# Attention with grouped queries: contiguous casts, rows transposed two at a time, and a shorter VectorE exponent

## Chip, cores, metric

One core of a Trainium2 chip. The metric is device time in microseconds (us); executions of a kernel lie within some 2% of each other, and each comparison uses the fast runs of both kernels made on the same chip in the same rounds. A profiled span is one execution's, and up to 6 us from the timed median of the same kernel.

## The reference

Eight batches, eight query heads in two groups, two key/value heads, sequence 1024, head dimension 64; softmax(q k^T / 8) v, in float32:

```python
scores = scale * np.matmul(q_group, k_group.transpose(0, 1, 3, 2))
scores_max = np.max(scores, axis=-1, keepdims=True)
attn = np.exp(scores - scores_max)
attn = attn / (np.sum(attn, axis=-1, keepdims=True) + 1e-08)
output[:, q_start:q_end, :, :] = np.matmul(attn, v_group)
```

## The kernel before

Scores are made transposed: a cell is one 128 x 512 block (128 keys, 512 queries), 8 cells a job, 128 jobs. A cell's exponents are made either by ScalarE (two cells at once, kind A) or by VectorE (kind D): a first pass writes bits from PSUM as uint16, and for four cells at once a chain of passes adds a quadratic correction. A small planner, run when the kernel is built, decides which cell goes where and in which order each engine works; transfers are recorded at "plan time of first use minus a lead". Parts that matter (cuts marked, and the chain in short form):

```python
def cast(key, src):                       # fp32 -> bf16, DRAM to DRAM, issued by GpSimd
    scr = scr_pool.tile([S, G * D], BF16, name="scr")
    nc.gpsimd.dma_start(out=scr.rearrange("s (g d) -> s g d", g=G),
                        in_=src.rearrange("g s d -> s g d"))      # runs of 64 elements
def transpose(key, dst, n):               # issued by SyncE
    nc.sync.dma_start_transpose(out=dst[:, rows], in_=scratch[key][rows, :])
def place_k(b, g):                        # GpSimd copies
    nc.gpsimd.tensor_copy(out=ksets[b % 2][half, g, :], in_=kT[b][half, :])
def place_v(b, g):
    nc.gpsimd.tensor_copy(out=vsets[b % 2][:, g, :, 0:D], in_=vstage.pop((b, g)))
...                                       # VectorE chain of four cells
    z = pd & 0xFF
    y = z * (CURVE_A / 512) + CURVE_B / 2
    y = z * y
    z = pd >> 1
    pd = z + y
```

The softmax here doesn't subtract the row's maximum and nothing guards it: scores larger than these inputs give would overflow.

## Time and profile before

| | before |
|---|---|
| time, us | 447.93 (447.81 to 448.04) |
| span of the profiled run, us | 449.2 |
| DVE (VectorE) / ACT (ScalarE) / PE (TensorE) busy | 93% / 87% / 86% |
| granted TensorE clock | 0.979 |

The prediction below shows the lines of this profile and reads them: VectorE is the bound, and it is lengthened where GpSimd works. Two more lines of it matter later, from the waits of GpSimd (what waited, for what; us in all, times, longest):

```profile
POOL vset L281 <- DMA vstage<-in_v_dram: 173.8, 7, 38.3
POOL vset L281 <- PE aps L324: 66.5, 2, 34.9
```

The trace shows GpSimd working in the order of its program: a query cast starts at 214.31 us, right behind the last of two value copies that had waited 31.6 us for TensorE's scores and 2.1 us for its output products. So the casts stood behind copies that waited for loads and for TensorE: the copies held the casts back, although nobody had asked them to.

### The profile page before, as it was taken

The page shows a single profiled execution, that of the slowest core. Times are in us where ns is not written, and L with a number is a line of the kernel's source. Part 1 is how long each engine was busy: PE and PEld are TensorE (multiplying, and loading weights), DVE is VectorE, ACT ScalarE, POOL GpSimd, SP SyncE. Part 2 cuts the span into 40 slices and gives each one's busy share as a digit, 9 for nine tenths or more (in the row PEclk, how much of TensorE's full clock was granted, in tenths as well). Part 3 has the DMA queues.
Part 4 walks back from the last instruction along what each step waited for, and adds up shares of the span by engine and source line. Part 5 has one row for each costly group of instructions (what it writes and reads, how often), then busy time and mean ns, then how long its engine had stood idle before and what let it go on. Part 6 is the DMA issues. An engine that isn't in the chain of part 4 may idle for free.

```text
span 449.2 us, 12594 instructions
## 1 busy us (share of the span) xinstructions
PE 386.4 (86%) x5136; PEld 234.2 (52%) x5136; DVE 416.8 (93%) x699; ACT 389.7 (87%) x417; POOL 111.3 (25%) x80
## 2 busy tenths in 40 slices
PE   1989878999689998898799998899989987998972
PEld 1445545655456555464455565546545655564661
DVE  2699999899999999999999999999999999999976
ACT  1799988899689998899799999899998998999940
POOL 7600263003620039000820035400380016100000
PEclk9999999899899999999999999999999999999986
DMA  9922579226992399934992359933999357923221
GB/s 163 110 44 43 114 99 157 61 63 106 114 135 63 64 136 120 116 73 101 105 153 57 76 110 109 130 75 80 135 105 109 83 112 100 111 58 71 61 49 35
DMA packets 210649, 42.77 MB, mean 95 GB/s; under 512 B 210592, under 2 KB 210592, under 8 KB 210592
## 3 DMA queue, kind: packets, MB, share of 16 engines
q1 hardware_dynamic: 132160, 32.01, 39.2%
q0 software_dynamic: 78432, 9.96, 37.5%
q8 instruction: 40, 0.66, 0.7%
q14 instruction: 17, 0.14, 0.1%
HBM read 25.17 MB, written 26.74 MB: 116 GB/s over the span
## 4 chain that ended last, share of the span: by engine, by line
DVE 55%; PE 20%; DMA 9%; ACT 6%; issue 6%; SPq 3%; POOL 1%; ACTq 0%; POOLq 0%; DVEq 0%
DVE pd L344 11%; DVE y L375 10%; DVE pd L387 9%; PE aps L324 9%; DMA qT<-scr 7%; PE ops L395 6%; DVE ost L410 6%; DVE y L365 6%; ACT pa L335 6%; DVE z L377 5%; PE dps L324 4%; DVE z L359 4%; DVE rec L408 3%; SPq L256 2%; DMA kT<-scr 1%
## 5 line engine op out<-in xcount | busy, mean ns | idle before, releaser
L335 ACT ACTIVATE pa<-aps 128x1024 bf16<-128x1024 f32 x415 | 387.4, 1044 | 32.5 <-PE aps L324 30.5
L324 PE MATMUL aps<-qT,kset 128*128 128x512 bf16 x830 | 250.0, 383 | 21.3 <-ACT pa L335 11.4
L395 PEld LDWEIGHTS <-pa 128*128 128x128 bf16 x3320 | 137.0, 99 | 65.1 <-DVE ost L410 11.5
L395 PE MATMUL ops<-vset,pa 128*128 128x65 bf16 x3320 | 145.7, 195 | 3.0 <-DVE ost L410 3.0
L344 DVE TENSOR_SCALAR pd<-dps 128x512 uint16<-128x512 f32 x194 | 126.0, 682 | 6.3 <-PE dps L324 6.2
L324 PEld LDWEIGHTS <-kset 128*128 128x128 bf16 x1024 | 85.6, 98 | 85.4 <-issue 41.8
L281 POOL CAST vset<-vstage 128x512 bf16<-128x512 f32 x16 | 18.2, 1140 | 242.3 <-DMA vstage<-in_v_dram 173.8
L248 POOL DMA_DIRECT2D scr<-in_q_dram x31 | 77.8, 2948 | 0.0
L324 PE MATMUL dps<-qT,kset 128*128 128x512 bf16 x194 | 65.2, 386 | 2.4 <-DMA qT<-scr 1.1
L375 DVE TENSOR_TENSOR y<-z,y 128x2048 f16<-128x2048 uint16 (+1 forms) x49 | 61.6, 1257 | 1.7
L387 DVE TENSOR_TENSOR pd<-z,y 128x2048 uint16<-128x2048 uint16 (+1 forms) x49 | 60.3, 1231 | 1.5
L395 PEld LDWEIGHTS <-pd 128*128 128x128 bf16 x776 | 32.1, 98 | 52.0 <-DVE pd L387 42.2
L395 PE MATMUL ops<-vset,pd 128*128 128x65 bf16 x776 | 38.2, 195 | 24.0 <-DVE pd L387 23.5
L410 DVE TENSOR_TENSOR ost<-ops,rec 128x256 f32<-128x256 f32 x128 | 54.4, 425 | 4.4
L359 DVE TENSOR_SCALAR z<-pd 128x2048 uint16<-128x2048 uint16 (+1 forms) x49 | 40.1, 818 | 0.0
L365 DVE TENSOR_SCALAR y<-z 128x2048 f16<-128x2048 uint16 (+1 forms) x49 | 39.7, 810 | 0.4
L377 DVE TENSOR_SCALAR z<-pd 128x2048 uint16<-128x2048 uint16 (+1 forms) x49 | 36.1, 736 | 1.7
L408 DVE RECIPROCAL rec<-ops 128x4 f32<-128x4 f32 x128 | 22.2, 174 | 6.9 <-PE ops L395 6.9
L248 POOL DMA_DIRECT2D scr<-in_k_dram x7 | 28.6, 4079 | 0.0
L265 POOL COPY kset<-kT 64x1024 bf16<-64x1024 bf16 x14 | 16.1, 1151 | 28.8 <-DMA kT<-scr 28.4
L301 PE MATMUL dps<-ident,h 128*128 128x128 bf16 x16 | 2.1, 309 | 8.3 <-DVE h L298 8.3
L307 ACT COPY qT<-dps 128x1024 bf16<-128x1024 bf16 x1 | 1.0, 1012 | 8.3 <-PE dps L301 8.3
(12 smaller groups left out, 10.6 us busy)
## 6 DMA issues: line engine op xcount, KB each, us to landing
out_dram<-ost SPq DMA_DIRECT2D x128, 128.0 KB, 2.7
scr<-in_q_dram POOLq DMA_DIRECT2D x31, 256.0 KB, 7.8
vstage<-in_v_dram SPq DMA_DIRECT2D x16, 256.0 KB, 4.4
qT<-scr SPq DMA_TRANSPOSE x124, 2.7
scr<-in_k_dram POOLq DMA_DIRECT2D x7, 256.0 KB, 10.1
f<-in_k_dram SPq DMA_DIRECT2D x2, 256.0 KB, 3.6
f<-in_q_dram SPq DMA_DIRECT2D x2, 256.0 KB, 4.7
kT<-scr SPq DMA_TRANSPOSE x28, 2.6
```

What stands on the lines that cost most here:

```text
L248: nc.gpsimd.dma_start(out=scr.rearrange("s (g d) -> s g d", g=G), in_=src.rearrange("g s d -> s g d"),)
L324: nc.tensor.matmul(dst, lhsT=ksets[b % 2][:, g, c * 128 : (c + 1) * 128], rhs=qT[(b, j)][:, qb * QBS : (qb + 1) * QBS], start=True, stop=True,
L335: nc.scalar.activation(out=pt[:, 0:m], in_=psum.pop(("A", n))[:, 0:m], func=AF.Exp, scale=scale)
L344: nc.vector.tensor_scalar(out=groups[g][:, slot], in0=psum.pop(cell), scalar1=bits_scale, scalar2=bits_bias, op0=ALU.mult, op1=ALU.add,)
L359: nc.vector.tensor_scalar(out=z, in0=pd, scalar1=0xFF, scalar2=None, op0=ALU.bitwise_and)
L365: nc.vector.tensor_scalar(out=y, in0=temps[g][0], scalar1=CURVE_A / 512.0, scalar2=CURVE_B / 2.0, op0=ALU.mult, op1=ALU.add,)
L375: nc.vector.tensor_tensor(out=y, in0=z, in1=y, op=ALU.mult)
L377: nc.vector.tensor_scalar(out=temps[g][0], in0=pd, scalar1=1, scalar2=None, op0=ALU.logical_shift_right,)
L387: nc.vector.tensor_tensor(out=pd, in0=z, in1=y, op=ALU.add)
L395: nc.tensor.matmul(ops_of[s][:, qs, :], lhsT=p_of[cell][:, qs * 128 : (qs + 1) * 128], rhs=vsets[b % 2][:, g, c, :], start=opens and qs == ...
L408: nc.vector.reciprocal(out=rec, in_=o[:, :, D])
L410: nc.vector.tensor_tensor(out=ost, in0=o[:, :, 0:D], in1=rec.unsqueeze(2).to_broadcast([128, NQS, D]), op=ALU.mult,)
```

## The change

Its intent: take the shift out of the VectorE chain (steps of 7 bits need none); make casts contiguous, a whole batch of queries in one; free GpSimd of copies, so that it doesn't lengthen VectorE; make the start shorter. A transpose now reads two sequence rows of one head as one row of 128, so a job is the even or the odd queries of a head, keys are held for both sides, and keys and values are placed by SyncE's DMAs. The diff is shortened:

```diff
-    LIVE_A, LIVE_D, PENDING = 24, 7, 8
+    LIVE_A, LIVE_D, PENDING, ONLY_A = 26, 6, 8, 14     # the last 14 cells on ScalarE
...
-    jobs = [(b, j, qb, g) ...]
+    jobs = [(b, h, side) for b in range(B) for h in range(H) for side in range(2)]
...
-        nc.gpsimd.dma_start(out=scr.rearrange("s (g d) -> s g d", g=G), in_=src.rearrange("g s d -> s g d"))
+        nc.gpsimd.dma_start(out=scr.rearrange("n (p f) -> (n p) f", f=1024),
+                            in_=src.rearrange("n (p s) d -> (n p) (s d)", s=1024 // D))
...
-    def place_k(b, g):
-        nc.gpsimd.tensor_copy(out=ksets[b % 2][half, g, :], in_=kT[b][half, :])
+    def place_k(b, g, side, parity):
+        nc.sync.dma_start(out=ksets[b % 2][side * D : (side + 1) * D, g, side, parity * HALF : ...],
+                          in_=kT[(b, g)][parity * D : (parity + 1) * D, :])
+    def place_v(b, g):      # two nc.sync.dma_start, even and odd rows, from the cast values
...
-        z = pd & 0xFF; y = z * (CURVE_A / 512) + CURVE_B / 2; y = z * y; z = pd >> 1; pd = z + y
+        z = pd & 0x7F; y = z * (CURVE_A / 128) + CURVE_B;     y = z * y;              pd = pd + y
...
+            at(th - 7.0 + n, transpose_q, b, h, n)        # leads: us of the plan ahead of first use
+            at(th - 13.0 + n, transpose_k, b, g, n)       # first head of a group
+            at(th - 8.5, place_k, b, g, side, parity); at(th - 6.0, place_v, b, g)
+            at(t0 - 28.0, cast_kv, b); at(t0 - 24.0, cast_q, b, 0, H)      # a whole batch
```

More of the change, by code (lines that the diff above doesn't have):

```diff
@@ L18, in make_plan @@
 def make_plan(nj, nkc):
-    QK, PV, EXP, P1, NORM = 0.214, 0.142, 0.925, 0.665, 0.64
-    CHAIN = (0.60, 0.60, 1.08, 0.60, 1.08)
+    QK, PV, EXP, P1, NORM = 0.214, 0.143, 0.925, 0.605, 0.57
+    CHAIN = (0.73, 0.73, 1.26, 1.26)
     FROM_PE, FROM_ACT, FROM_DVE = 0.28, 0.18, 0.12
-    LIVE_A, LIVE_D, PENDING = 24, 7, 8
+    LIVE_A, LIVE_D, PENDING, ONLY_A = 26, 6, 8, 14
     INF = 1e9
@@ L53, in make_plan @@
                 ta = max(pe, min(a_free))
-            if pending < PENDING and (cur or live["D"] < LIVE_D):
+            if pending < PENDING and nxt < n - ONLY_A and (cur or live["D"] < LIVE_D):
                 td = max(pe, min(bank))
@@ L70, in make_plan @@
                 best = min(best or (INF,), (max(dve, q[0][0]), p, kind, 0))
-        if cur and nxt >= n and not p1q:
+        if cur and nxt >= n - ONLY_A and not p1q:
             best = min(best or (INF,), (dve, 9, "flush", 0))
@@ L180 @@
     G = k.shape[1]
-    NPAIR = H // G
+    HPG = H // G
     NKC = S // 128
     QBS = 512
-    NQB = S // QBS
+    HALF = S // 2
+    NHC = NKC // 2
     NQS = QBS // 128
@@ L188 @@
     scale = 1.0 / math.sqrt(D)
-    bits_scale = 256.0 * scale * math.log2(math.e)
-    bits_bias = 256.0 * 127.0
-    jobs = [
-        (b, j, qb, g)
-        for b in range(B)
-        for j in range(NPAIR)
-        for qb in range(NQB)
-        for g in range(G)
-    ]
+    bits_scale = 128.0 * scale * math.log2(math.e)
+    bits_bias = 128.0 * 127.0
+    jobs = [(b, h, side) for b in range(B) for h in range(H) for side in range(2)]
     plan = make_plan(len(jobs), NKC)
@@ L205 @@
     scr_pool = ctx.enter_context(
-        tc.tile_pool(name="scr", bufs=4, space=bass.MemoryType.DRAM)
+        tc.tile_pool(name="scr", bufs=2, space=bass.MemoryType.DRAM)
     )
     first_pool = ctx.enter_context(tc.tile_pool(name="firstp", bufs=1))
-    qT_pool = ctx.enter_context(tc.tile_pool(name="qTpool", bufs=4))
+    qT_pool = ctx.enter_context(tc.tile_pool(name="qTpool", bufs=6))
     kT_pool = ctx.enter_context(tc.tile_pool(name="kTpool", bufs=2))
-    vstage_pool = ctx.enter_context(tc.tile_pool(name="vstage", bufs=2 * G))
-    pa_pool = ctx.enter_context(tc.tile_pool(name="papool", bufs=24))
-    pd_pool = ctx.enter_context(tc.tile_pool(name="pdpool", bufs=7))
+    vstage_pool = ctx.enter_context(tc.tile_pool(name="vstage", bufs=G))
+    pa_pool = ctx.enter_context(tc.tile_pool(name="papool", bufs=26))
+    pd_pool = ctx.enter_context(tc.tile_pool(name="pdpool", bufs=6))
     tmp_pool = ctx.enter_context(tc.tile_pool(name="tmppool", bufs=2))
@@ L234 @@
         vsets.append(vs)
-        ks = const_pool.tile([128, G, S], BF16, name=f"kset{s}")
-        for g in range(G):
-            nc.gpsimd.memset(ks[(1 - g) * D : (2 - g) * D, g, :], 0.0)
+        ks = const_pool.tile([128, G, 2, S], BF16, name=f"kset{s}")
+        for side in range(2):
+            nc.vector.memset(ks[(1 - side) * D : (2 - side) * D, :, side, :], 0.0)
         ksets.append(ks)
@@ L242, with cast @@
     scratch = {}
-    vstage = {}
-    def cast(key, src):
-        scr = scr_pool.tile([S, G * D], BF16, name="scr")
+    def cast(key, src, n):
+        scr = scr_pool.tile([n, S * D], BF16, name=f"scr_{key[0]}{n}")
         nc.gpsimd.dma_start(
-            out=scr.rearrange("s (g d) -> s g d", g=G),
-            in_=src.rearrange("g s d -> s g d"),
-        )
-        scratch[key] = scr
+            out=scr.rearrange("n (p f) -> (n p) f", f=1024),
+            in_=src.rearrange("n (p s) d -> (n p) (s d)", s=1024 // D),
+        )
+        return scr
@@ L254, in transpose, with cast_q, cast_kv @@
+    def cast_q(b, h, n):
+        scr = cast(("q",), q[b, h : h + n], n)
+        for i in range(n):
+            scratch[("q", b, h + i)] = scr[i]
+    def cast_kv(b):
+        for name, src in (("k", k), ("v", v)):
+            scr = cast((name,), src[b], G)
+            for g in range(G):
+                scratch[(name, b, g)] = scr[g]
     def transpose(key, dst, n):
         rows = slice(n * PIECE, (n + 1) * PIECE)
-        nc.sync.dma_start_transpose(out=dst[:, rows], in_=scratch[key][rows, :])
@@ L258, in transpose_k @@
-    def transpose_k(b, n):
+        src = scratch[key].rearrange("(r c) -> r c", c=2 * D)
+        nc.sync.dma_start_transpose(out=dst[:, rows], in_=src[rows, :])
+    def transpose_k(b, g, n):
         if n == 0:
-            kT[b] = kT_pool.tile([128, S], BF16, name="kT")
-        transpose(("k", b), kT[b], n)
-    def place_k(b, g):
-        half = slice(g * D, (g + 1) * D)
-        nc.gpsimd.tensor_copy(out=ksets[b % 2][half, g, :], in_=kT[b][half, :])
-    def transpose_q(b, j, n):
-        if n == 0:
-            qT[(b, j)] = qT_pool.tile([128, S], BF16, name="qT")
-        transpose(("q", b, j), qT[(b, j)], n)
@@ L272, in load_v, with transpose_q @@
-    def load_v(b):
+            kT[(b, g)] = kT_pool.tile([128, HALF], BF16, name="kT")
+        transpose(("k", b, g), kT[(b, g)], n)
+    def place_k(b, g, side, parity):
+        nc.sync.dma_start(
+            out=ksets[b % 2][
+                side * D : (side + 1) * D, g, side, parity * HALF : (parity + 1) * HALF
+            ],
+            in_=kT[(b, g)][parity * D : (parity + 1) * D, :],
+        )
+    def transpose_q(b, h, n):
+        if n == 0:
+            qT[(b, h)] = qT_pool.tile([128, HALF], BF16, name="qT")
+        transpose(("q", b, h), qT[(b, h)], n)
@@ new lines, in place_v, with first_loads @@
+    def place_v(b, g):
+        for two in range(2):
+            nc.sync.dma_start(
+                out=vsets[b % 2][:, g, two * NHC : (two + 1) * NHC, 0:D],
+                in_=scratch[("v", b, g)].rearrange(
+                    "(c p two d) -> two p c d", p=128, two=2, d=D
+                )[two],
+            )
+    def first_loads():
+        staged = []
+        for eng, src in ((nc.sync, k[0, 0]), (nc.scalar, q[0, 0])):
+            f = first_pool.tile([128, NHC, 2, D], FP32, name=f"f{len(staged)}")
+            eng.dma_start(
+                out=f, in_=src.rearrange("(c p two) d -> p c two d", p=128, two=2)
+            )
+            staged.append(f)
@@ L273, in load_v @@
         for g in range(G):
-            vf = vstage_pool.tile([128, NKC, D], FP32, name="vstage")
+            vf = vstage_pool.tile([128, NHC, 2, D], FP32, name="vstage")
             nc.sync.dma_start(
-                out=vf, in_=v[b, g].rearrange("(c p) d -> p c d", p=128)
+                out=vf, in_=v[0, g].rearrange("(c p two) d -> p c two d", p=128, two=2)
             )
-            vstage[(b, g)] = vf
-    def place_v(b, g):
-        nc.gpsimd.tensor_copy(out=vsets[b % 2][:, g, :, 0:D], in_=vstage.pop((b, g)))
@@ L283, in first_transposes @@
-    def first_transposes():
-        srcs = (k[0], q[0, 0::NPAIR])
-        staged = []
-        for n, src in enumerate(srcs):
-            f = first_pool.tile([128, NKC, G, D], FP32, name=f"f{n}")
-            for g in range(G):
-                nc.sync.dma_start(
-                    out=f[:, :, g, :],
-                    in_=src[g].rearrange("(c p) d -> p c d", p=128),
-                )
-            staged.append(f)
-        qT[(0, 0)] = qT_pool.tile([128, S], BF16, name="qT")
-        for n in range(2):
-            h = first_pool.tile([128, NKC, G * D], BF16, name=f"h{n}")
-            nc.vector.tensor_copy(out=h, in_=staged[n].rearrange("p c g d -> p c (g d)"))
-            tp = dbanks[n].tile([128, S], BF16, name=f"dps{n}")
-            for c in range(NKC):
-                nc.tensor.transpose(tp[:, c * 128 : (c + 1) * 128], h[:, c, :], ident)
-            if n == 0:
-                for g in range(G):
-                    half = slice(g * D, (g + 1) * D)
-                    nc.vector.tensor_copy(out=ksets[0][half, g, :], in_=tp[half, :])
-            else:
-                nc.scalar.copy(out=qT[(0, 0)], in_=tp)
+            for two in range(2):
+                nc.gpsimd.tensor_copy(
+                    out=vsets[0][:, g, two * NHC : (two + 1) * NHC, 0:D],
+                    in_=vf[:, :, two, :],
+                )
@@ new lines, in first_loads @@
+        fk, fq = staged
+        hk = first_pool.tile([128, NHC, 3, D], BF16, name="hk")
+        nc.vector.tensor_copy(out=hk[:, :, 0:2, :], in_=fk)
+        nc.vector.tensor_copy(out=hk[:, :, 2, :], in_=fk[:, :, 0, :])
+        hq = first_pool.tile([128, NHC, 2 * D], BF16, name="hq")
+        nc.scalar.copy(out=hq, in_=fq.rearrange("p c two d -> p c (two d)"))
+        tk = dbanks[0].tile([128, 2, HALF], BF16, name="dps0")
+        tq = dbanks[1].tile([128, HALF], BF16, name="dps1")
+        for w in range(2):
+            for c in range(NHC):
+                nc.tensor.transpose(
+                    tk[:, w, c * 128 : (c + 1) * 128],
+                    hk[:, c, w : w + 2, :].rearrange("p w d -> p (w d)"),
+                    ident,
+                )
@@ new lines, in first_loads @@
+        for c in range(NHC):
+            nc.tensor.transpose(tq[:, c * 128 : (c + 1) * 128], hq[:, c, :], ident)
+        qT[(0, 0)] = qT_pool.tile([128, HALF], BF16, name="qT")
+        lo, hi = slice(0, D), slice(D, 2 * D)
+        nc.vector.tensor_copy(out=ksets[0][lo, 0, 0, 0:HALF], in_=tk[lo, 0, :])
+        nc.scalar.copy(out=qT[(0, 0)], in_=tq)
+        nc.vector.tensor_copy(out=ksets[0][lo, 0, 0, HALF:S], in_=tk[lo, 1, :])
+        nc.vector.tensor_copy(out=ksets[0][hi, 0, 1, 0:HALF], in_=tk[hi, 1, :])
@@ L309 @@
+        nc.vector.tensor_copy(out=ksets[0][hi, 0, 1, HALF:S], in_=tk[hi, 0, :])
     p_of = {}
@@ L315, in score @@
     def score(cell, kind, n, slot, col):
-        b, j, qb, g = jobs[cell // NKC]
+        b, h, side = jobs[cell // NKC]
         c = cell % NKC
@@ L325, in score @@
             dst,
-            lhsT=ksets[b % 2][:, g, c * 128 : (c + 1) * 128],
-            rhs=qT[(b, j)][:, qb * QBS : (qb + 1) * QBS],
+            lhsT=ksets[b % 2][:, h // HPG, side, c * 128 : (c + 1) * 128],
+            rhs=qT[(b, h)],
             start=True,
@@ L359, in exp_curve @@
             nc.vector.tensor_scalar(
-                out=z, in0=pd, scalar1=0xFF, scalar2=None, op0=ALU.bitwise_and
+                out=z, in0=pd, scalar1=0x7F, scalar2=None, op0=ALU.bitwise_and
             )
@@ L367, in exp_curve @@
                 in0=temps[g][0],
-                scalar1=CURVE_A / 512.0,
-                scalar2=CURVE_B / 2.0,
+                scalar1=CURVE_A / 128.0,
+                scalar2=CURVE_B,
                 op0=ALU.mult,
@@ L375, in exp_curve @@
             nc.vector.tensor_tensor(out=y, in0=z, in1=y, op=ALU.mult)
-        elif step == 3:
-            nc.vector.tensor_scalar(
-                out=temps[g][0],
-                in0=pd,
-                scalar1=1,
-                scalar2=None,
-                op0=ALU.logical_shift_right,
-            )
         else:
-            z, y = temps.pop(g)
+            y = temps.pop(g)[1]
             groups.pop(g)
-            nc.vector.tensor_tensor(out=pd, in0=z, in1=y, op=ALU.add)
+            nc.vector.tensor_tensor(out=pd, in0=pd, in1=y, op=ALU.add)
     def output_mms(s, cell, opens, closes, bk):
-        b, j, qb, g = jobs[s]
+        b, h, side = jobs[s]
         c = cell % NKC
@@ L397, in output_mms @@
                 lhsT=p_of[cell][:, qs * 128 : (qs + 1) * 128],
-                rhs=vsets[b % 2][:, g, c, :],
+                rhs=vsets[b % 2][:, h // HPG, c, :],
                 start=opens and qs == 0,
@@ L404, in normalise @@
     def normalise(s):
-        b, j, qb, g = jobs[s]
+        b, h, side = jobs[s]
         o = ops_of.pop(s)
@@ L416, in normalise @@
         nc.sync.dma_start(
-            out=out[b, j + g * NPAIR].rearrange("(s p) d -> p s d", p=128)[
-                :, qb * NQS : (qb + 1) * NQS, :
-            ],
+            out=out[b, h].rearrange("(s p two) d -> two p s d", p=128, two=2)[side],
             in_=ost,
@@ L435 @@
         at(op[0], run[op[1]], *op[2:])
-    per_pair = NQB * G
     for b in range(B):
-        t0 = first_use[b * NPAIR * per_pair]
-        if b > 0:
-            at(t0 - 24.0, cast, ("k", b), k[b])
-            for n in range(S // PIECE):
-                at(t0 - 12.0 + 0.7 * n, transpose_k, b, n)
-            for g in range(G):
-                at(t0 - 5.0 + g, place_k, b, g)
-            at(t0 - 16.0, load_v, b)
-            for g in range(G):
-                at(t0 - 11.0 + 3.0 * g, place_v, b, g)
-        for j in range(NPAIR):
-            if b == 0 and j == 0:
-                continue
-            tj = first_use[(b * NPAIR + j) * per_pair]
-            if b > 0 or j > 1:
-                at(max(tj - 21.0, -1.0), cast, ("q", b, j), q[b, j::NPAIR])
-            for n in range(S // PIECE):
-                at(tj - 7.0 + 0.7 * n, transpose_q, b, j, n)
-    with tc.manual_schedule():
-        cast(("q", 0, 1), q[0, 1::NPAIR])
-        first_transposes()
-        load_v(0)
-        for g in range(G):
-            place_v(0, g)
+        for h in range(H):
+            if b == 0 and h == 0:
+                continue
+            th = first_use[(b * H + h) * 2]
+            for n in range(HALF // PIECE):
+                at(th - 7.0 + n, transpose_q, b, h, n)
+            if h % HPG == 0:
+                g = h // HPG
+                for n in range(HALF // PIECE):
+                    at(th - 13.0 + n, transpose_k, b, g, n)
+                for side in range(2):
+                    for parity in range(2):
+                        at(th - 8.5, place_k, b, g, side, parity)
+                if b > 0:
+                    at(th - 6.0, place_v, b, g)
+        if b > 0:
+            t0 = first_use[b * H * 2]
+            at(t0 - 28.0, cast_kv, b)
+            at(t0 - 24.0, cast_q, b, 0, H)
+    with tc.manual_schedule():
+        first_loads()
+        cast_q(0, 1, HPG - 1)
+        cast_kv(0)
+        cast_q(0, HPG, HPG)
         for _, _, f, args in sorted(events, key=lambda e: e[:2]):
```

## The prediction

> **What bounds the kernel now.** I read the page's busy line first, then the groups with shapes kept apart, then the waits, and then the timeline of VectorE beside that of GpSimd.
>
> ```profile
> PE 386.4 (86%) x5136; PEld 234.2 (52%) x5136; DVE 416.8 (93%) x699; ACT 389.7 (87%) x417; POOL 111.3 (25%) x80
> ```
>
> Three engines lie at 86% to 93%. The slices of the page show DVE at 9 in nearly every slice from the second to the last but one. The waits view settles who is the bound: who waits for DVE, and how little DVE waits itself.
>
> ```profile
> PEld L395 <- DVE pd L387: 42.2, 41, 3.1
> ACT pa L335 <- PE aps L324: 30.5, 42, 2.3
> DVE rec L408 <- PE ops L395: 6.9, 10, 1.8
> DVE pd L344 <- PE dps L324: 6.2, 4, 4.5
> ```
>
> DVE waited 6.9 + 6.2 us, and 4.5 us of that is before its first exponent. ACT waited 30.5 us for scores, TensorE 42.2 us for VectorE's exponents. So DVE is the bound; its first exponent is at 13.77 us and its last instruction ends at 446.1 us, a stretch of 432.3 us.
>
> The groups and the timeline give its costs (columns of a group: busy us, mean ns; of the timeline: start, length):
>
> ```profile
> L359 DVE TENSOR_SCALAR z<-pd 128x2048 uint16<-128x2048 uint16 x48 | 39.7, 826 | 0.0
> L365 DVE TENSOR_SCALAR y<-z 128x2048 f16<-128x2048 uint16 x48 | 39.2, 818 | 0.4
> L377 DVE TENSOR_SCALAR z<-pd 128x2048 uint16<-128x2048 uint16 x48 | 35.7, 743 | 1.7
> ```
>
> ```profile
> 191.86 0.68 DVE L365 TENSOR_SCALAR y<-z 128x2048 f16<-128x2048 uint16 x1
> 192.58 1.23 DVE L375 TENSOR_TENSOR y<-z,y 128x2048 f16<-128x2048 uint16 x1
> 193.84 0.69 DVE L377 TENSOR_SCALAR z<-pd 128x2048 uint16<-128x2048 uint16 x1
> 194.56 1.23 DVE L387 TENSOR_TENSOR pd<-z,y 128x2048 uint16<-128x2048 uint16 x1
> 195.71 1.28 DVE L344 TENSOR_SCALAR pd<-dps 128x512 uint16<-128x512 f32 x2
> 196.91 0.17 DVE L408 RECIPROCAL rec<-ops 128x4 f32<-128x4 f32 x1
> ...
> 117.31 1.50 DVE L359 TENSOR_SCALAR z<-pd 128x2048 uint16<-128x2048 uint16 x1
> 118.85 2.11 DVE L365 TENSOR_SCALAR y<-z 128x2048 f16<-128x2048 uint16 x1
> ```
>
> ```profile
> 116.13 2.13 POOL L265 COPY kset<-kT 64x1024 bf16<-64x1024 bf16 x2 [5.35 <-DMA kT<-scr]
> 118.21 4.22 POOL L248 DMA_DIRECT2D scr<-in_q_dram  x2
> ```
>
> The reader is to see two lengths for one instruction: 0.68 us where GpSimd rests (around 192 us it does), 1.50 and 2.11 us where GpSimd copies the keys or writes the descriptors of casts. The means 826 and 818 ns of the groups mix both. Starts give the undisturbed step, which is what counts on a full engine: y 0.72, product 1.26, shift 0.72, sum 1.15, first pass (195.71 to 196.91, two of them) 0.60 each, a normalisation pair 0.54 (196.91 to 197.45); z is 0.59 or 0.72 by what follows, taken as 0.66.
>
> The budget of before, 194 cells on DVE in 48.5 groups of four: first pass 194 x 0.60 = 116.4; z 32.0; y 34.9; product 61.1; shift 34.9; sum 55.8; norm 128 x 0.54 = 69.1. Together 404.2 us. With waits of 8.6 us (6.9 + 6.2 - 4.5) this leaves 432.3 - 404.2 - 8.6 = 19.5 us of lengthening. The means against the medians of the tile view (z 826 - 684, y 818 - 684, product 1268 - 1226, shift 743 - 694, sum 1242 - 1226 ns) add up to 383 ns a group, or 18.6 us in 48.5 groups: the same amount by another way, so the budget closes.
>
> **What the Trainium skill says.** "VectorE: DVE Perf Modes", The perf-mode tier table, has 693 ns for a one-source and 1224 ns for a two-source 16-bit operation on 2048 elements; the trace agrees (0.68 to 0.69, and 1.23 us). So the shift is worth one one-source pass a group, and the new sum, again of one uint16 and one fp16 tensor, costs what the old one did. "SBUF — State Buffer", Who interferes with whom, says that VectorE and GpSimd share one pair of ports under an exclusive lock; "DMA: Bandwidth & Descriptors", SWDGE vs HWDGE vs iDMA, adds that GpSimd writes the descriptors of its DMAs into SBUF itself, while those issued from SyncE don't pass there. The trace agrees: it is these passes that lengthen. The latter section also has each DMA engine go round robin between the two kinds by packets; the trace of before, all small packets, can't show what large ones do to that.
>
> **The change, part by part.**
>
> 1. The shift goes. The order of the changed program has 200 cells on DVE in 50 groups with four passes (ACT has 412 pair exponents, not 415). New budget: 200 x 0.60 = 120.0; z 33.0; y 36.0; product 63.0; sum 57.5; norm 69.1; together 378.6 us, 25.6 less. (Shift -34.9, six more cells +9.3.)
>
> 2. GpSimd is emptied. Its 14 key copies and 14 of its 16 value casts go to SyncE's DMAs. Casts fall from 38, of 2048 packets each, to 25 contiguous ones (four for the first batch, then three a batch). In before they filled GpSimd for 106 us (77.8 + 28.6). With far fewer descriptors I take 3 us of lengthening on DVE in place of 19.5: 16.5 less. The 3 is my choice, one short collision of about 0.12 us a cast.
>
> 3. DMA load. Page part 3 has 78,432 packets on the software queue at 37.5% of 16 engines: 0.375 x 16 x 449.2 us / 78,432 = 34 ns for 128 bytes. Nearly all that goes. It bounds nothing now. SyncE issues more: 156 transposes x 1.23 us, 128 outputs x about 0.45 and some 88 small placements x about 0.5 are 294 us of 410, so it keeps pace, but a head's two transposes need 2 x 1.23 + 2.7 (landing) = 5.2 us of their 7 us lead.
>
> 4. The start. Before, TensorE's first score is at 11.44 us: keys for both groups land at 5.26, two casts and two copies of 0.7 us each on DVE stand in series with cold transposes (1.03 us), then a 1.01 us copy on ACT. Now one head of q and k is loaded, on two queues, the query's cast goes to ACT and all copies have 512 columns. DVE has four memsets first (by the skill, VectorE page, Zero memsets can be issued as uint32, one element a cycle; 1024 words each, an estimate of 4.4 us, so to about 5.2 us). Then key cast 0.45 + 0.3, transposes 1.1, copy 0.45, or ACT's way of like length: first score near 8.3 us and DVE's first pass near 10.5, 3.3 earlier.
>
> 5. Against that, head 1 needs the cast of its queries, which GpSimd now issues after four value copies that wait for loads: issue near 8.6 us, landing near 15.5, transposes landed near 18.5 to 19.5, against a need near 14.5 (two jobs after the first score). I charge 4 us of this stall.
>
> 6. The tail. The last 14 cells go to ACT, so the last chain no longer stands behind the last first pass. Waits of DVE in the tail stay about 4.5 us (scores, output products, normalisation), and 3.1 us from DVE's last instruction to the end as before.
>
> The sum: 10.5 + 378.6 + 3 (GpSimd) + 4 (head 1) + 8 (waits in between, a little above the 5.4 of before outside the tail, as DVE is less alone) + 4.5 + 3.1 = 411.7 us of span. The timed median lies 1.3 us under the span (447.9 against 449.2): **about 411 us**.
>
> **The rivals.**
>
> - **Three engines of one length.** ACT needs 412 x 0.91 = 375 us (seven exponents in 6.52 us), DVE 382, and TensorE's matmuls lay at 386 busy before. In order and with two score buffers each, they may hold each other up: if ACT keeps the 31 us it waits now, the end is near 9.3 + 375 + 31 + 8 = 423. For it: ACT loses 3 us in 60 even in the quiet stretch 300 to 360 us. Against: most of that is TensorE behind DVE.
> - **Large casts delay transposes.** Once a batch 3 MB are read in one burst; a head's transposes have under 2 us to spare. If each of seven batches costs 4 us of stall, 439. For: TensorE waited for query transposes already (6.3 us). Against: small packets of before held the engines at 9 of 10 for longer, and still landed in 2.7 us.
> - **The lengthening stays**, if it hangs on the transfers and not on GpSimd's work: 411 + 16 = 427. Against: the 1.50 and 2.11 us lie within GpSimd's instructions.
>
> **Range and chances.** All three rivals still leave the removed pass in hand, so slower is remote; the second at full size is the only way to within 2% (439 and up). A better case (no head-1 stall, no extra waits) is 411 - 4 - 6 = 401. Range 400 to 426.
>
> **What would show it.** Right: DVE still the fullest engine, z and y means near 690 ns, four passes a group, a first exponent of ACT near 9.3 us, a hole of about 4 us for a query transpose within the first 20 us, ACT waits near 20 us. Wrong: z and y means still above 800 ns; DVE under 90% with TensorE waiting on query transposes or key placements at each batch; a lower granted clock (now 0.979) with TensorE full.

## The result

The changed kernel takes 475.27 us (474.67 to 475.88), a ratio of 1.061 (95% interval 1.055 to 1.067): slower by 6%. Here and below a ratio is the mean time of one kernel's fast runs over that of the other's of the same rounds, so not quite the ratio of the medians quoted.

First the busy line of the changed kernel's page, and three rows of its 40 slices (11.8 us each; tenths):

```profile
PE 376.9 (80%) x5043; PEld 237.7 (50%) x5132; DVE 381.5 (81%) x666; ACT 384.4 (81%) x415; POOL 14.7 (3%) x37
...
DVE  6200137999999798899989999999898989879995
...
PEclk9755577999999899899999999999999999989999
DMA  6999982334342533444344444343524444343423
```

VectorE's busy time fell by 35 us (416.8 to 381.5) and the span rose by 24. For most of slices 2 to 5 (11.8 to 59 us) every engine stands and only the DMA engines work. The granted clock (PEclk) is low at the start (0.55 from 13.7 to 54.7 us, where TensorE does nothing) and 0.99 from 90 us on: a lower clock with TensorE full, which the prediction named as a sign of being wrong, is not what happened. Next the groups of the two one-source passes (busy, mean ns):

```profile
L393 DVE TENSOR_SCALAR y<-z 128x2048 f16<-128x2048 uint16 x50 | 34.3, 687 | 0.6
L387 DVE TENSOR_SCALAR z<-pd 128x2048 uint16<-128x2048 uint16 x50 | 34.2, 684 | 0.0
```

826 and 818 ns have become 684 and 687: the lengthening is gone. Then the waits, and one line of the chain of waits:

```profile
PE aps L352 <- DMA qT<-scr_q: 63.3, 16, 41.2
DVE pd L372 <- PE dps L352: 54.9, 15, 41.4
```

```profile
13.66 41.08 DMA qT<-scr_q
```

TensorE stood 41.2 us for one transpose, the second of head 1's two, and every other engine with it; a second such hole (8.4 us) follows at 62 us. GpSimd's own waits show what filled the DMA engines:

```profile
POOL scr_v L243 <- DMA scr_q<-in_q_dram: 20.8, 6, 4.4
...
POOL scr_q L243 <- DMA scr_k<-in_k_dram: 4.6, 6, 0.8
```

It waits only for its own earlier casts to land. With the copies gone nothing holds it back, and it issues the casts of all eight batches one after the other; the last lands at 69.6 us. The DMA view of the window 13.7 to 54.7 us (queue, packets, MB, share of 16 engines; then issues with the median us to landing):

```profile
q0 software_dynamic: 635, 8.72, 99.6%
q1 hardware_dynamic: 603, 0.14, 2.2%
...
qT<-scr_q SPq DMA_TRANSPOSE x5, 52.1
```

Casts (q0) took 99.6% of 16 engines; SyncE's queue (q1) got 603 packets of 256 bytes or less through beside 635 of the casts. The trace's packet records give 16 to 32 KB as written, and 1.2 to 2.4 us, for one cast packet: the rows of 1024 elements had been merged into runs of 8192 to 16384. A transpose is 256 packets, 16 on each engine, and about one passed for each cast packet.

VectorE's time in one line each, from the instruction records (first pass until, work, gaps over 0.15 us, end after its last instruction; they sum to the span):

| | start | work | gaps | end | span |
|---|---|---|---|---|---|
| before | 13.8 | 423.8 | 8.5 | 3.1 | 449.2 |
| predicted | 10.5 | 381.6 | 16.5 | 3.1 | 411.7 |
| after | 10.2 | 385.4 | 74.3 | 2.9 | 472.8 |

The whole error sits in the gaps: 49.8 us in the two holes and 24.5 in small ones, the largest of them near the borders of batches and groups (2.6 us at 187 us, 2.3 at 413).

### The profile page after: what moved, and what is told of

The parts are those of the page before. It is cut to its first block, busy times and chain, and to the rows that moved or that the text cites. A ratio compares the mean times of both kernels' runs of the same rounds, so it can differ in the third digit from the quotient of the medians.

```text
span 472.8 us, 12507 instructions
## 1 busy us (share of the span) xinstructions
PE 376.9 (80%) x5043; PEld 237.7 (50%) x5132; DVE 381.5 (81%) x666; ACT 384.4 (81%) x415; POOL 14.7 (3%) x37
## 4 chain that ended last, share of the span: by engine, by line
ACT 26%; DVE 24%; DMA 21%; PE 19%; issue 5%; SPq 3%; another core or an unknown queue 2%; POOL 0%; ACTq 0%; DVEq 0%
ACT pa L363 26%; DMA qT<-scr_q 17%; PE aps L352 11%; DVE pd L372 6%; PE ops L415 5%; DVE y L403 4%; DVE ost L430 4%; DVE pd L407 3%; DVE y L393 3%; PE dps L352 3%; DVE z L387 2%; DVE rec L428 2%; SPq L263 2%; DMA out_dram<-ost 1%
## 5 line engine op out<-in xcount | busy, mean ns | idle before, releaser
L363 ACT ACTIVATE pa<-aps 128x1024 bf16<-128x1024 f32 x412 | 382.0, 1056 | 75.3 <-remote 43.0
L352 PE MATMUL aps<-qT,kset 128*128 128x512 bf16 x735 | 231.3, 387 | 80.4 <-DMA qT<-scr_q 63.3
L372 DVE TENSOR_SCALAR pd<-dps 128x512 uint16<-128x512 f32 x200 | 130.1, 682 | 55.2 <-PE dps L352 54.9
L407 DVE TENSOR_TENSOR pd<-pd,y 128x2048 uint16<-128x2048 uint16 x50 | 61.2, 1225 | 1.7
L403 DVE TENSOR_TENSOR y<-z,y 128x2048 f16<-128x2048 uint16 x50 | 61.2, 1225 | 1.7
L415 PEld LDWEIGHTS <-pd 128*128 128x128 bf16 x800 | 39.0, 98 | 29.4 <-DVE pd L407 7.1
L415 PE MATMUL ops<-vset,pd 128*128 128x65 bf16 x800 | 45.7, 195 | 0.9
L428 DVE RECIPROCAL rec<-ops 128x4 f32<-128x4 f32 x128 | 22.7, 177 | 21.6 <-PE ops L415 20.7
L393 DVE TENSOR_SCALAR y<-z 128x2048 f16<-128x2048 uint16 x50 | 34.3, 687 | 0.6
L387 DVE TENSOR_SCALAR z<-pd 128x2048 uint16<-128x2048 uint16 x50 | 34.2, 684 | 0.0
L243 POOL DMA_DIRECT2D scr_q<-in_q_dram x9 | 4.7, 527 | 4.6 <-DMA scr_k<-in_k_dram 4.6
L243 POOL DMA_DIRECT2D scr_v<-in_v_dram x8 | 3.9, 486 | 20.8 <-DMA scr_q<-in_q_dram 20.8
```

Of the source, the lines that this page charges most:

```text
L243: nc.gpsimd.dma_start(out=scr.rearrange("n (p f) -> (n p) f", f=1024), in_=src.rearrange("n (p s) d -> (n p) (s d)", s=1024 // D),)
L352: nc.tensor.matmul(dst, lhsT=ksets[b % 2][:, h // HPG, side, c * 128 : (c + 1) * 128], rhs=qT[(b, h)], start=True, stop=True,)
L363: nc.scalar.activation(out=pt[:, 0:m], in_=psum.pop(("A", n))[:, 0:m], func=AF.Exp, scale=scale)
L372: nc.vector.tensor_scalar(out=groups[g][:, slot], in0=psum.pop(cell), scalar1=bits_scale, scalar2=bits_bias, op0=ALU.mult, op1=ALU.add,)
L387: nc.vector.tensor_scalar(out=z, in0=pd, scalar1=0x7F, scalar2=None, op0=ALU.bitwise_and)
L393: nc.vector.tensor_scalar(out=y, in0=temps[g][0], scalar1=CURVE_A / 128.0, scalar2=CURVE_B, op0=ALU.mult, op1=ALU.add,)
```

## The experiments

Fifteen kernels; all gave correct results. Ratios are to the kernel before. Times are medians of all four runs; one run each of e7, e10, e11 and e15 was slow and is in no ratio.

| kernel | us | ratio (95%) |
|---|---|---|
| e1 paced | 471.76 | 1.053 (1.045 to 1.061) |
| e2 runs of 1024 | 462.0 | 1.030 (1.021 to 1.039) |
| e3 both | 460.53 | 1.027 (1.019 to 1.035) |
| e4 before, VectorE part only | 430.29 | 0.961 (0.953 to 0.969) |
| e5 runs of 256 | 450.7 | 1.006 (0.997 to 1.015) |
| e6 casts by head | 438.44 | 0.980 (0.973 to 0.988) |
| e7 casts by head, early leads | 401.95 | 0.895 (0.888 to 0.903) |
| e8 layout part only | 483.25 | 1.079 (1.070 to 1.088) |
| e9 early leads only | 452.05 | 1.008 (1.000 to 1.015) |
| e10 early leads, paced batch casts | 446.12 | 0.990 (0.981 to 1.000) |
| e11 as e7, large packets | 441.79 | 0.982 (0.972 to 0.991) |
| e12 as e7, VectorE part of before | 422.32 | 0.942 (0.936 to 0.948) |
| e13 as e11, placements by GpSimd | 399.55 | 0.890 (0.885 to 0.896) |
| e14 early leads, runs of 256 | 427.62 | 0.952 (0.947 to 0.957) |
| e15 as e11, more lead | 436.0 | 0.970 (0.963 to 0.977) |

**e1, pacing.**

```diff
+    def pace():                 # GpSimd waits for ScalarE's latest exponents
+        nc.gpsimd.tensor_copy(out=tick, in_=last["pa"][:, 0, 0:64])
+            at(t0 - 28.0, pace)
             at(t0 - 28.0, cast_kv, b)
+            at(t0 - 24.0, pace)
             at(t0 - 24.0, cast_q, b, 0, H)
```

> The changed kernel with one small GpSimd copy of an exponent tile ahead of the key/value casts and ahead of the query cast of each batch from the second on, so that GpSimd issues them when ScalarE has got that far (28 and 24 us of the plan ahead), as its value and key copies did by accident before. Theory A (the hole of 41.4 us in the trace after is made by all casts of all batches running at once, from 7 to 70 us, ahead of the transposes): the hole shrinks to the 4 us or so that the four casts of the first batch make, the second of 8.4 us goes, 475 - 37 - 8 = 430 us or a little less. Rival B (large packets are harmful in any amount): each later batch has a burst of 7 us in which a transpose crawls, some 4 us each, 7 batches: about 455 us. Rival C (the hole has another cause, such as SyncE's queue): stays at 475 us.

Measured 471.76. The 41 us hole is gone (4.1 us of VectorE's gap there), and yet the time hardly moved. The waits of e1:

```profile
ACT pa L370 <- PE aps L358: 69.2, 43, 10.4
PE aps L358 <- DMA qT<-scr_q: 47.0, 18, 9.9
```

VectorE's gaps now stand at 93 (4.8 us), 151 to 161 (10.1), 212 (5.5), 269 (4.9), 323 (4.8) and 378 us (5.0). So the holes moved to the casts, and mostly to those of keys and values, 512 KB a batch: TensorE's wait in five of these six ends within 1.2 us after they have landed (95.3, 214.1, 269.3, 325.1, 380.3 us), and in two of the five the query cast had not yet been issued (217, 384 us). Only the hole at 151 us lasts until a query cast lands (159.2). Theory A in its first form (all at once is the harm) falls. Rival B's time (455) is the nearest, and still too mild; that the size of the packets is the reason, as B has it, is not shown, since e3 has its holes at the same places with small ones.

**e2, the packets.**

```diff
-            out=scr.rearrange("n (p f) -> (n p) f", f=1024),
+            out=scr.rearrange("n (x y f) -> y (n x) f", y=16, f=1024),     # same permutation in in_
```

> The changed kernel with its casts cut into runs of 1024 elements (4 KB read, 2 KB written) in place of 8192 to 16384; not paced, so still all in one burst, of the same bytes. Theory A in its sharp form (a DMA engine takes cast and transpose packets in turn, so that a transpose's 16 packets an engine wait for about 16 cast packets): a cast packet falls from 1.2 to 2.4 us to about 0.2 to 0.3 us, a transpose lands in 5 to 7 us in place of 21 to 55, the hole shrinks to 5 us or so, 430 to 438 us in all. Rival (the bytes of the burst count, not the size of a packet): the engines are as full for as long, the hole stays above 30 us, 465 us or more.

Measured 462.0: the same bytes, still in one burst. The DMA view of e2 for 13.7 to 24 us:

```profile
q0 software_dynamic: 1021, 1.96, 100.7%
q1 hardware_dynamic: 718, 0.17, 12.8%
...
qT<-scr_q SPq DMA_TRANSPOSE x5, 12.8
```

The engines are as full, but transposes land in 12.8 us in the median, not 52.1; in the trace one lands every 3.05 us, just half of the 6.2 us for which a head lasts. The hole is 10 us, and two more of 11 and 12 us follow. Packet size matters, but the 430 to 438 us of theory A were not reached.

**e3, both.** The two edits above together.

> Both edits together: runs of 1024 elements and paced casts. Theory A: a little better than either, 418 to 428 us, what my sum gave (411) plus the stalls at the group borders that the trace after shows apart from the two holes. If it is no better than the paced one, packet size matters only where casts pile up; if it is no better than the small one, pacing is worth nothing once packets are small.

Measured 460.53, no better than e2 alone: six holes of 3.9 to 5.3 us stay beside the casts of keys and values, even in packets of 2 KB as written, where these come within the 7 us lead of a transpose.

**e4, the VectorE part alone**, in the kernel before: the planner, the chain and the two buffer counts of the change; everything else of before.

> The kernel before with the VectorE part and the plan of the change alone (steps of 7 bits, no shift, 200 cells on VectorE, the last 14 on ScalarE), its layout, casts, copies on GpSimd left as they were. If my budget of VectorE holds: start 13.8, work 378.6, lengthening by GpSimd still near 19, waits 13, end 3: 427 us of span, about 426 timed. If the removed pass is not on the path that sets the end (another engine takes over at once): 440 or more. z and y means should stay above 800 ns here.

Measured 430.29 (span 425.7). Start 13.8, work 399.4, gaps 9.4, end 3.1. The work is 378.6 as budgeted, plus 20.8 that GpSimd still adds here (z and y means 808 and 832 ns). So the VectorE part of the prediction holds, and VectorE's work did lie on the path that sets the end. The pass, the six more cells and the last 14 cells on ScalarE were not tried apart.

**e5, runs of 256**, the edit of e2 with `f=256`.

> As the second experiment (not paced), with runs of 256 elements (1 KB read, 512 bytes written). Theory D, formed from the first four runs: a DMA engine takes one packet of the cast queue, then one of SyncE's queue, in turn, so a transpose of 16 packets an engine costs 16 turns, each as long as a cast packet. With 16 to 32 KB packets that was 21 to 41 us for one transpose, with 4 KB packets the transposes landed every 3.05 us (190 ns a turn), just what a head needs in its 6.2 us. With 1 KB packets a turn is 50 to 80 ns, a transpose costs 1.3 us more at most, SyncE's issue (1.24 us) is the limit again: the holes of 10 to 12 us go, one of some 3 us at head 1 stays, 425 to 432 us. Rival (the bytes of the burst, whatever their packets): no better than the 462 us of the second experiment.

Measured 450.7. The DMA view for 15 to 30 us:

```profile
q0 software_dynamic: 4554, 2.29, 111.9%
q1 hardware_dynamic: 2304, 0.53, 28.6%
...
qT<-scr_q SPq DMA_TRANSPOSE x5, 6.8
```

52.1, 12.8 and 6.8 us for packets of 16 to 32 KB, 2 KB and 512 bytes (as written): in the order that taking turns gives, but not in proportion (theory D had some 4 us); e14 below shows why. The two cast packets for each of SyncE's are a mean over a window in part of which SyncE's queue was empty. The better part of the gain that theory D promised did not come: gaps of 3 to 7 us stay as long as the burst lasts. Here full engines cost something even with packets of 512 bytes.

**e6 and e7, casts by head.** In e6 each head's queries are cast by themselves in runs of 1024, paced, 16 us ahead; keys and values of a group 22 us ahead; head 1's cast is issued before the value copies. e7 adds earlier leads (and casts 18 and 26 us ahead in place of 16 and 22):

```diff
-   at(th - 7.0 + n, transpose_q, ...)      at(th - 13.0 + n, transpose_k, ...)
-   at(th - 8.5, place_k, ...)              at(th - 6.0, place_v, ...)
+   at(th - 10.0 + n, transpose_q, ...)     at(th - 19.0 + n, transpose_k, ...)
+   at(th - 14.0, place_k, ...)             at(th - 11.0, place_v, ...)
```

> The changed kernel with the casts made one head at a time (128 KB out, runs of 1024 elements, 4 packets an engine), each paced by ScalarE 16 us of the plan ahead of the head's first use (keys and values of a group 22 us ahead), and head 1's cast issued ahead of the value copies. Theory D: a cast in the way of a transpose now costs at most 4 turns, 0.8 us, below what the transposes have to spare, so no hole stays at a cast; the start has none either. What is left are waits at the group borders, where SyncE stands in line behind the keys' transposes and placements (1 to 3 us each, 15 borders): 412 to 422 us. If the batch bursts are not the cause of the 5 us holes in the first and third experiment, those stay: 440 or more.

> As e6_heads, and SyncE's work is recorded earlier: query transposes 10 us ahead (7), key transposes 19 (13), key placements 14 (8.5), value placements 11 (6), casts 18 and 26 (16 and 22). If the waits at the group borders are SyncE's line, they go: 405 to 414 us, near the sum of my prediction without its head-1 stall. If they are something else (full chip memory, ScalarE, TensorE), no gain over e6_heads.

Measured 438.44 and 401.95. In e6 no gap of VectorE is over 5 us, but 37.6 us are lost in small ones; the leads were worth more than I had thought; which of them (transposes, placements or casts) did it was not tried apart. In e7 6.2 us are left: start 10.2, work 381.9, gaps 6.2, end 2.9. The waits and the busy line of e7:

```profile
PE 372.5 (93%) x5132; PEld 233.7 (58%) x5132; DVE 378.6 (94%) x666; ACT 381.8 (95%) x415; POOL 87.4 (22%) x178
```

```profile
ACT pa L375 <- PE aps L363: 5.5, 6, 1.3
...
PE aps L363 <- DMA qT<-scr_q: 4.1, 4, 1.4
```

63.3 us of TensorE's wait for queries have become 4.1, and three engines run at 93 to 95%.

**e8, the layout part alone**: the changed kernel with the chain, plan and buffer counts of before.

> The changed kernel with VectorE's part and the plan of before (steps of 8 bits with the shift, 194 cells on VectorE): the layout and the casts alone. The two parts should add up: the VectorE part was worth 17 us in the kernel before (fourth experiment), the layout part loses what is left, 475 - 430 = 45, so 447.5 + 45 = 492 us if they add; less, 478 to 485, if VectorE is short of the bound now and then here, as GpSimd no longer lengthens its passes.

Measured 483.25, gaps of 51.3 us in two holes. The two parts don't quite add (492): freed of GpSimd's lengthening, VectorE had 406.1 us of work here and not 423.8.

**e9, early leads alone**, the edit of e7's leads on the changed kernel, casts untouched.

> The changed kernel with SyncE's work recorded earlier as in e7 (query transposes 10 us ahead, key transposes 19, placements 14 and 11) and nothing else: casts by batch, in 16 to 32 KB packets, not paced. The two holes of the start stay (41 and 8 us), since no lead helps a transpose that takes 21 to 41 us; the waits at the group borders after 80 us (ACT loses some 20 us there in the trace after) go: 475 - 15 to 20 = 455 to 460 us. If the lead alone makes e7's gain: near 410.

Measured 452.05. The waits of e9:

```profile
PE aps L352 <- DMA qT<-scr_q: 50.0, 2, 41.7
DVE pd L372 <- PE dps L352: 45.9, 6, 41.9
```

Two holes and nothing else: after 90 us VectorE's gaps are 2.5 us (20.9 in the changed kernel). So, of what the changed kernel loses against e7, about 23 us go by the leads and the 49 us between e9 and e7 (450.1 and 401.2 of span) by the casts. In the other order, casts first (e6) and leads then, it is 37 and 35 us of span: the split is not clean, as each hides a part of the other.

**e10**, e1's pacing with the early leads.

> e1_paced with the same early leads: a burst of 7 to 9 us in large packets a batch, but transposes with 3 us more to spare. Theory D: the burst stops transposes for as long as it lasts, so the hole of 4 to 5 us at each of seven batches shrinks by 3 us and the border waits go: 470 - 20 - 18 = 432 us, give or take 8. If it reaches e7 (402), lead is all that matters and per-head casts do nothing; if it stays above 455, lead doesn't help where a burst stands in the way.

Measured 446.12 (one of its four runs, the profiled one, was slow). Lead helps, but does not cover a batch's burst: worse than expected (432, give or take 8), and 43 us behind e7 by the means of the fast runs. SyncE's issues took 376 us here too, so that the bursts and its line (e11) are not told apart.

**e11**, e7 with each head's cast left contiguous (16 packets of 8 KB as written, one an engine).

> e7 with each head's cast left contiguous (16 packets of 16 KB read, one an engine) in place of runs of 1024 elements: does the size of a packet matter when a cast is one packet an engine? Theory D: a transpose meets one turn of about 1.2 us at most, or none, which the 10 us lead hides: 402 us as e7. If large packets harm in themselves (by a long hold on the chip's memory, say): 410 or more.

Measured 441.79, where theory D had 402. Its turns are not what failed: transposes landed as fast as in e7 (3.5 and 3.4 us in the median). But SyncE's issues, added up from the trace, took 378 us of 438 against 334 of 401. TensorE waits for transposes again (4.1 us in e7), and a new wait shows, of VectorE for output buffers that SyncE has not yet sent off:

```profile
PE aps L361 <- DMA qT<-scr_q: 27.6, 14, 6.0
...
DVE ost L440 <- DMA out_dram<-ost: 13.3, 7, 4.3
```

**e13 and e15**, to tell why. e13 is e11 with `nc.gpsimd.dma_start` for the 88 placements; e15 is e11 with 5 us more lead for all and 8 query buffers.

> e11 (per-head casts in one 16 KB packet an engine, 438 us against e7's 402) with the 88 placements of keys and values issued by GpSimd in place of SyncE. In e11 the transposes landed as fast as in e7 (median 3.5 against 3.4 us), but SyncE spent 378 us issuing against 334, its issues drawn out. Theory E: SyncE's in-order line is what large packets lengthen, and at 378 us of issue and its waits it no longer keeps its lead. Taking some 50 us of issue off it brings e11 back to 402 to 412 us. Rival F (the delay is in the transfers themselves): no better than 430.

> e11 with 5 us more lead for everything and two more query buffers. Under theory E (SyncE's line too full) more lead helps only in part: 415 to 435. Under rival F (single transfers too late), the lead covers it: 402 to 410.

Measured 399.55 and 436.0. More lead only moves the wait, in e15 to the outputs that stand behind the early transposes in SyncE's line:

```profile
DVE ost L440 <- DMA out_dram<-ost: 33.9, 10, 5.3
PE ops L425 <- DVE ost L440: 25.3, 11, 4.3
```

Less work on the line (306 us of 398) cures it, with the large packets still there. TensorE's wait in e13:

```profile
PE aps L361 <- DMA qT<-scr_q: 1.2, 2, 0.9
```

Query transposes land no faster than in e11 (3.9 us in the median), and yet VectorE's gaps are 3.5 us in all; GpSimd, busy 137.8 us, does not lengthen z (685 ns). So theory E, the line of SyncE, fits, and rival F does not. One doubt stays: GpSimd now also waits 63.6 us ahead of placements, and this spaces its casts otherwise, which was not tried apart. e13 is the fastest kernel, 11% under the kernel before and level with e7 within the intervals of their ratios.

**e14**, early leads and runs of 256, all casts in one burst.

> The changed kernel with early leads and runs of 256 elements, all casts still by batch and in one burst at the start: no pacing at all. If turn taking by packets is the mechanism and the rest is lead, the burst is harmless here: e5's later holes at 46 to 95 us (3 to 6 us each) go, about 7 us at head 1 stay: 402 + 7 to 12 = 409 to 414 us. If the bytes of the burst hurt whatever the packets, 430 or more.

Measured 427.62, between the two answers: 7.4 us at head 1 and some 19 us in gaps from 59 to 102 us, when the burst draws to its end; after it hardly anything. The slowest tenth of the query transposes took 8.1 us or more to land. The packet records tell what the size of the packets does and what it does not. First the changed kernel from 34 to 54.7 us, then e14 from 65 to 90 us, both with work in both queues throughout:

```profile
q0 software_dynamic: 295, 4.19, 94.6%
q1 hardware_dynamic: 295, 0.07, 2.2%
...
q0 software_dynamic: 6401, 3.23, 93.5%
q1 hardware_dynamic: 6403, 1.42, 47.8%
```

One packet passes for one (in e2 1227 and 1229 from 19 to 32 us), so theory D's turns are shown: in the changed kernel, e2 and e14 the 256 packets of the first transpose take 16.0, 2.6 and 1.6 us from the first to the last, against 0.4 in e7. But that transpose's first packet starts 3.8, 4.3 and 4.0 us after SyncE began to issue it, against 1.3 in e7 and in the kernel before: this part does not shrink with the packets, and theory D had left it out. What makes it is not shown.

**e12, the VectorE part again**, taken out of e7.

> e7 with VectorE's part and the plan of before (8-bit steps with the shift, 194 cells): what the VectorE part is worth where transfers cost nothing. My budget: 404 us of work against 379, start and tail alike but 3 us worse in the tail (the last cells on VectorE): 402 + 25 + 3 = 430 us; not as much, some 422, if other engines set part of e7's time. And against before it shows what the layout part is worth when its transfers are hidden: 447.5 to about 428, the start (3 us), the lengthening by GpSimd (17 us) and no more.

Measured 422.32; VectorE's work is 404.8 us (the budget of before without lengthening: 404.2) and its gaps 2.7. So with transfers hidden the layout part as e7 has it (casts by head, early leads) is worth 28.8 us of span, 449.2 - 420.4 (start 3.8, lengthening 19.0, gaps 5.8, end 0.2), and the VectorE part 19.2 more (420.4 - 401.2).

## Why the prediction was wrong, point by point

- **VectorE is the bound and the pass is on its path: right.** e4 and e12 show it, to within 1.5 us of the budgets (399.4 against 378.6 + 19.5; 404.8 against 404.2).
- **GpSimd's lengthening goes: right**, 142 ns a z pass to nothing; the 3 us I allowed were not needed.
- **The start, step 4: right** (first pass at 10.2 us, 10.5 predicted). The four memsets took 0.91 us each, less than the estimate from the skill (4.4 us for four), and with the gaps between them just the 4.4 us, from 1.01 to 5.41. The tail, step 6: 1.8 us of gaps in VectorE's last 10 us, 4.5 predicted.
- **Step 5, head 1's stall, failed**: 4 us predicted, 41.4 and then 8.4 measured. I took the landing of a transpose, 2.7 us, from a profile with 128-byte cast packets and only added SyncE's issue. The cast itself landed at 12.3 us, earlier than my 15.5; it was the transposes, landing at 34.0 and 54.7, that stood between the packets of later casts.
- **Step 3, "it bounds nothing now", failed with it.** I counted packets and bytes and saw both fall. I did not ask when the casts would be issued once GpSimd had nothing to wait for, nor what one packet of 16 to 32 KB does to a queue that takes turns with it, although the prediction quotes the skill on these turns: 16 turns of 1.2 to 2.4 us are 20 to 39 us (an estimate from the packet times above), and head 1's first transpose landed 21.6 us after its issue, the second 20.7 us after the first. The built order of GpSimd showed the casts standing alone; the question was answerable before the run.
- **Waits in between: 8 us predicted, some 20 measured after 90 us.** e9 removes them by lead alone. I had SyncE issue for 294 us; it was 370: 48 in three transposes stuck in the hole, the others 1.35 us each in the mean (1.23 assumed), placements 0.58.
- **The second rival named the mechanism** (large casts delay transposes) but not the place or size: 28 us in seven bursts. Spread like that (e1) it costs more, 57.7 us of gaps after 90 us, 35.1 of them in six holes, most of which stand at the key and value casts.
- **The first rival** (three engines of one length) did not come about: ACT waits for TensorE for 5.5 us in e7, with all three at 93 to 95%.

My sum without its stall and extra waits was 401 ("a better case"); e7 has 401.95. The working of the compute engines was sound, that of the transfers was not.

Open: why large packets draw out SyncE's issue (e11) even when a cast has one packet an engine; and why a transpose's first packet stands some 4 us in every burst of contiguous casts, whatever their packets, but not in the kernel before, whose casts in packets of 128 bytes were running then too.

## What to carry to other kernels

Before you take work off an in-order engine that also issues DMAs, ask what its waits were holding back: here copies had spaced the casts, and without them 62 us of transfers ran ahead of a transpose needed at once. In this kernel a transfer on the path needed short neighbours, a lead with room for them (7 us were too few in e6, 10 enough in e7), and an issuing engine with slack; the kernels that lack one of the three (e9, e6, e11) took 35 to 49 us more of span than the one that has all (e7), which beats the kernel before by 10%. Take a transfer's landing time from a profile only if its neighbours stay as they are.

## What the Trainium skill lacked or had wrong

- "DMA: Bandwidth & Descriptors", SWDGE vs HWDGE vs iDMA, gives a packet as at most 4096 bytes by preference and as the point where an engine changes queues. Here the contiguous cast went in records of 16 to 32 KB, 1.2 to 2.4 us each, and transposes beside them took up to 55 us to land, against 2.7 in the median before. The page doesn't say what a larger packet does to the queue beside it; and no page was found that tells of the 3.8 to 4.3 us before a transpose's first packet in such a burst (1.3 before).
- The same page, Rules for kernel authors, advises to coalesce many small transfers into one large one (it speaks of those under 64 KB), and has no word on urgent transfers beside the large one. Here 1 MB casts by batch (e10, 446.1 us) lost to 128 KB casts by head in runs of 1024 (e7, 402.0) with the same leads. How much of it is the size is not shown: contiguous casts by head (e11) came to 441.8, and to 399.6 once SyncE had less to issue (e13).
- The same page, Issuing engines are not separate DMA queues, calls the issue time that another engine saves usually small relative to the DMA itself. Here that is so of one transfer (0.74 us of issue, 2.4 us to landing for keys in e11), but on a line nearly full it decided: moving 88 small placements from SyncE to GpSimd brought 441.8 us to 399.6.
